# Moving two row-sum matmuls down TensorE's order, and rounding the weight block A22 ahead of the differences S3 and S4

## The chip, the cores and the metric

The kernel runs on one core of a Trainium2 chip. A core has five engines that run side by side and wait for each other by semaphores: TensorE (PE, matmuls and transposes; its weight loads are listed as PEld), VectorE (DVE), ScalarE (ACT), GpSimd (POOL) and SyncE (SP, which issues the DMA transfers). The metric is the device time of one execution in microseconds; the time of a kernel is the median of its runs.

## The reference

One step of a diffusion backbone with one layer. There are 128 context tokens and 512 latent tokens of 1024 features, in float32. What bears on the change:

```python
h = _rms(x, norm_mix) * (1 + sc1) + sh1
proj = h @ w_in                       # q, k, v, and the three conv inputs gb, gc, u
attn = _block_attention(q_r, k_all, v_all)
y_conv = gb * _short_conv(gc * u, conv_w)
merged = concat([_rms(attn, attn_out_norm), _rms(y_conv, conv_out_norm)])
x = x + g1 * (merged @ w_out)
h2 = _rms(x, norm_ffn) * (1 + sc2) + sh2
gate, up = split(h2 @ w_gate_up)      # 1024 -> 2 * 2816
x = x + g2 * ((silu(gate) * up) @ w_down)
```

`_rms(attn, ...)` needs, for each token, the sum of squares of the 512 attention features. It is that sum, for two tiles of tokens, that the change moves.

## The kernel before, in words

**Tokens and precision.** The 640 tokens are five tiles of 128: tiles 0 to 3 latent, tile 4 context. A float32 matmul is done as three matmuls of rounded operands (helper `mm3`, lines 155 to 157): each operand is split into a high half (`wh`, rounded by ScalarE, line 151) and a low half (`wl`, the rest, by VectorE, line 152). High half first, then low half, then TensorE can use the block.

**Who sets the order.** TensorE's order is written out by hand for the whole kernel. For the other engines a scheduler sets the order from dependences and priorities (`early(...)`), except in the first stage, and for VectorE in the opening of the feed-forward part (the block of `f == 0`), where it is by hand too. Tiles come from rings of a few buffers; a new tile waits until the last reader of the buffer it takes is done. Each engine works through its queue strictly in order, so an instruction that waits holds up everything behind it.

**The attention stage** is the list `SEQ`. Its steps:
- `Sn.h`: scores of unit n (one of 16: token tile, key/value head, head pair), head h, on TensorE into a score buffer (line 835); VectorE takes the maximum (841), ScalarE the exponential with its sum (845), then the scaling (847 to 851). There is one score buffer.
- `Tn.g`: transposes of the probabilities of both heads (line 862) into a tile `pt` of the PSUM pool "t", which has two buffers (`PT = 2`); ScalarE and VectorE split it into `ph` and `pl`.
- `On.g`: the product with the values (line 879). After the last one ScalarE copies the result out (886), two DMAs swap halves (894, 895), VectorE adds (900, 901), ScalarE squares into `osq` (902), and GpSimd adds the squares over features in two steps (905, 906).
- `rt`: `att_rms(t)`, line 954. Two passes of a matmul of `osq` with a column of ones give the sums of squares of token tile t, in a tile of the pool "t"; VectorE scales it (line 163, `ms`) and GpSimd takes the power -1/2 (line 165, `rA`). `rA[t]` is first used in the next stage, where the output projection is scaled.
- `F1`: one piece of a filler that runs the conv projections (lines 723 to 725) and the remaining adaLN products (line 394) through the same stage. `Qt`, `qt`: turn and split the queries.

Token tile 0 is finished by unit 3, tile 2 by unit 11.

**The feed-forward part** multiplies the gate and up weights with h2 by Winograd's variant of Strassen's method: 22 blocks f of 128 gate and 128 up columns, of which blocks 0 and 1 are done plainly and blocks 2 to 21 by seven products of 12 matmuls each. In TensorE's order these are A11 B11, S1 T1, S2 T2, A12 B21, S3 T3, S4 B22, A22 T4 (functions `ff_a`, `ff_c`, `ff_d`, `ff_b`, `ff_e`). Between them lie copies on ScalarE that TensorE needs: of the first product (line 1219), of S1 T1 (p5) and S2 T2 (u), line 1212, and after S3 T3 the copy b4 (line 1241), into which A22 T4 is added. The outputs are put together on VectorE (1243, 1246, 1251, 1253) and ScalarE (1225, 1252), and split for the down product (gT).

The raw gate block g(f) and up block u(f) are loaded by SyncE (line 228) into a ring `wf` of three buffers. `op_load` then makes, in the order of `PRODS`:
- "A1": the split of g itself, "A22": the split of half of u;
- "S12": the sums S1 = A21 + A22 and S2 = S1 - A11 on VectorE (line 206) into a tile `sx`, then its split;
- "S34": S3 = A11 - A21 and S4 = A12 - S2 in place in the same `sx` (line 206), then its split.

The halves live in two rings of four buffers, `wh` and `wl`. "A22" takes one buffer, holding both its halves, from `wh` for even f and from `wl` for odd f; the others take one of each. The order of `PRODS` is thus also the order of the rings. Rounding runs ahead of TensorE by up to six entries of that list (`AOP = 6`).

After each group of blocks (0 to 5, 6 to 11, 12 to 16, 17 to 21) comes the down product, whose weights pass through the same rings.

Of the kernel before, what the change touches and what calls it, by code (L numbers as in the profile page):

```python
# [49 lines left out]
GCUT = [0, 6, 12, 17, 22]  # L50
GB = 3
# [40 lines left out]
def build(ctx, tc, x_prompt, x_sample, c, cache_k, cache_v, c_ctx, norm_mix, norm_ffn, w_ada, b_ada,  # L92
# [195 lines left out]
            plan(("ada", 5, j, kp), wa[:, 2 * kp:2 * kp + 2, 5 * D + j * 512:5 * D + (j + 1) * 512], 2, "f")  # L288

    GROUPS = [list(range(a, b)) for a, b in zip(GCUT, GCUT[1:])]  # L290
    PLAIN, PRODS = ("A1", "A2"), ("A1", "S12", "S34", "A22")
    PAIRS = {"A11": ("A1", 0), "A12": ("A1", 4), "A21": ("A2", 0), "A22": ("A2", 4),
             "S1": ("S12", 0), "S2": ("S12", 4), "S3": ("S34", 0), "S4": ("S34", 4)}

# [1038 lines left out]


tile_hymba = with_exitstack(build)

_INS = ["x_prompt", "x_sample", "c", "cache_k", "cache_v", "c_ctx", "norm_mix", "norm_ffn", "w_ada", "b_ada",
# [44 lines left out]
```

## Time and profile before

| | |
|---|---|
| median of 3 runs (lowest to highest) | 755.55 us (754.55 to 755.95) |
| the profiled execution | 756.18 us |
| its span, first to last instruction | 754.4 us |
| TensorE busy | 732.7 us (97%) |
| VectorE / ScalarE / GpSimd busy | 530.2 / 374.9 / 49.5 us |
| granted TensorE clock | 1.00 |
| moved by DMA | 84.50 MB |

The attention stage runs from about 64 to 256 us, the output projection from 256 to 325 us, the feed-forward part from there to the end. In rows of the timeline stand: start, duration, engine, line, operation, output and inputs with the buffer numbers left out, and in brackets the engine's idle time before it and what ended it. In rows of the waits stand: who waited for whom, microseconds in all, times, longest. In rows of the stages: the stage, its length, then busy time and instructions of PE, PEld, DVE, ACT and POOL, the granted clock, the DMA share and GB/s. Matmuls are pipelined, so the durations of neighbours overlap; what counts is the distance of starts.

### The profile page before, as it was taken

Reading aid. Unit: us, or ns where it says so; the run is one execution under the profiler, and the core shown is the slowest. Engines: PE = TensorE matmul, PEld = TensorE weight load, DVE = VectorE, ACT = ScalarE, POOL = GpSimd, SP = SyncE. Lnnn points to the kernel's source line nnn. Section 1 sums busy time; section 2 is a strip of 40 time slices with the busy share of each in tenths; the row PEclk is TensorE's granted clock in tenths of the full one; section 3 lists DMA queues with packets and bytes.
Section 4 is the critical chain, followed back from the end, with each engine's and each line's share of the span. In section 5 each row is a group of like instructions: output and inputs, shape, how many; then the busy total and the mean of one; then the engine's idle time right before and its main releaser. Section 6 shows DMA issues by size and latency. Waiting matters only on the chain.

```text
span 754.4 us, 11635 instructions
## 1 busy us (share of the span) xinstructions
PE 732.7 (97%) x4556; PEld 657.7 (87%) x4556; DVE 530.2 (70%) x905; ACT 374.9 (50%) x701; POOL 49.5 (7%) x85
## 2 busy tenths in 40 slices
PE   7999999999989999999899999999999999999997
PEld 5568878988988887899898799999889998899986
DVE  5558878676656798787868768774568766677653
ACT  5356777677666534775552225553125551255510
POOL 2403101011010120100000000000000000000000
PEclk9999999999999999999999999999999999999999
DMA  9985133533522464031225313233112232123312
GB/s 289 288 244 163 45 109 100 167 93 93 173 92 91 133 226 137 1 112 48 87 91 181 113 56 97 72 99 125 56 56 84 84 112 83 45 72 110 99 70 84
DMA packets 101387, 84.50 MB, mean 112 GB/s; under 512 B 3502, under 2 KB 81650, under 8 KB 101332
## 3 DMA queue, kind: packets, MB, share of 16 engines
q1 hardware_dynamic: 100980, 83.39, 35.9%
q0 software_dynamic: 352, 0.37, 0.3%
q8 instruction: 36, 0.59, 0.3%
q14 instruction: 19, 0.16, 0.1%
HBM read 79.68 MB, written 2.75 MB: 109 GB/s over the span
## 4 chain that ended last, share of the span: by engine, by line
PE 78%; DVE 7%; DMA 6%; ACT 5%; issue 2%; SPq 1%; POOL 1%; ACTq 0%; DVEq 0%
PE pf L155 17%; PE pf L156 17%; PE pf L157 17%; PE pc L723 3%; PE pc L724 3%; PE pc L725 3%; PE ps L835 2%; PE po L879 2%; PE pt L862 2%; DMA es<-t 2%; PE pc L394 2%; DMA af<-in_w_ada_dram 2%; DMA wf<-in_w_gate_up_dram 1%; PE ph L156 1%; PE ph L157 1%
## 5 line engine op out<-in xcount | busy, mean ns | idle before, releaser
L152 DVE TENSOR_TENSOR wl<-wf,wh 128x1024 fp32r<-128x1024 f32 (+1 forms) x58 | 68.7, 1185 | 59.1 <-ACT wh L151 44.6
L151 ACT ACTIVATE wh<-wf 128x1024 fp32r<-128x1024 f32 (+1 forms) x68 | 65.6, 968 | 86.2 <-PE pf L157 45.6
L155 PE MATMUL pf<-B,wh 128*128 128x320 f32 x288 | 89.3, 310 | 0.0
L157 PE MATMUL pf<-B,wl 128*128 128x320 f32 x288 | 89.3, 310 | 0.0
L156 PE MATMUL pf<-B,wh 128*128 128x320 f32 x288 | 89.2, 310 | 0.0
L155 PE MATMUL pf<-T,wh 128*128 128x320 f32 x280 | 86.9, 310 | 2.2 <-ACT pf L1241 1.6
L155 PE MATMUL pf<-wh,gT 128*128 128x512 f32 (+1 forms) x225 | 87.0, 387 | 0.0
L157 PE MATMUL pf<-T,wl 128*128 128x320 f32 x280 | 86.7, 310 | 0.0
L156 PE MATMUL pf<-T,wh 128*128 128x320 f32 x280 | 86.7, 310 | 0.0
L156 PE MATMUL pf<-wl,gT 128*128 128x512 f32 (+1 forms) x225 | 86.6, 385 | 0.0
L157 PE MATMUL pf<-wh,gT 128*128 128x512 f32 (+1 forms) x225 | 86.6, 385 | 0.0
L151 ACT ACTIVATE wh<-sx 128x1024 fp32r<-128x1024 f32 x40 | 42.4, 1060 | 82.9 <-PE pf L157 49.8
L152 DVE TENSOR_TENSOR wl<-sx,wh 128x1024 fp32r<-128x1024 f32 x40 | 48.9, 1224 | 27.4 <-ACT wh L151 23.8
L723 PE MATMUL pc<-hH,wh 128*128 128x320 f32 x192 | 61.2, 319 | 0.0
L724 PE MATMUL pc<-hL,wh 128*128 128x320 f32 x192 | 59.4, 309 | 0.0
L725 PE MATMUL pc<-hH,wl 128*128 128x320 f32 x192 | 59.4, 309 | 0.0
L155 PEld LDWEIGHTS pf<-T,wh 128*128 128x128 f32 x280 | 52.6, 188 | 2.7 <-ACT pf L1241 1.8
L157 PEld LDWEIGHTS pf<-B,wl 128*128 128x128 f32 x288 | 54.1, 188 | 0.1
L155 PEld LDWEIGHTS pf<-B,wh 128*128 128x128 f32 x288 | 54.1, 188 | 0.1
L156 PEld LDWEIGHTS pf<-B,wh 128*128 128x128 f32 x288 | 54.1, 188 | 0.1
L156 PEld LDWEIGHTS pf<-T,wh 128*128 128x128 f32 x280 | 52.6, 188 | 0.0
L157 PEld LDWEIGHTS pf<-T,wl 128*128 128x128 f32 x280 | 52.6, 188 | 0.0
(302 smaller groups left out, 1672.2 us busy)
## 6 DMA issues: line engine op xcount, KB each, us to landing
wf<-in_w_gate_up_dram SPq DMA_DIRECT2D x44, 512.0 KB, 3.8
aw<-in_w_ada_dram SPq DMA_DIRECT2D x24, 512.0 KB, 3.9
wf<-in_w_down_dram SPq DMA_DIRECT2D x20, 512.0 KB, 3.9
wf<-in_w_in_dram SPq DMA_DIRECT2D x18, 512.0 KB, 6.1
af<-in_w_ada_dram SPq DMA_DIRECT2D x32, 256.0 KB, 6.4
x<-in_x_sample_dram SPq DMA_DIRECT2D x8, 512.0 KB, 6.1
wf<-in_w_out_dram SPq DMA_DIRECT2D x8, 512.0 KB, 4.2
wf<-in_w_ada_dram SPq DMA_DIRECT2D x8, 512.0 KB, 3.8
```

Source lines behind the costliest of these rows:

```text
L151: act.activation(hi, src, AF.Copy)
L152: dve.tensor_tensor(lo, src, f32(hi), ALU.subtract)
L155: pe.matmul(out, lh, rh, start=start, stop=False, skip_group_check=more)
L156: pe.matmul(out, lh, rl, start=False, stop=False, skip_group_check=more)
L157: pe.matmul(out, ll, rh, start=False, stop=stop, skip_group_check=more)
L394: pe.matmul(out[CG * g:CG * (g + 1)], cp[:, k], w, start=(k < 4), stop=(k >= KD - 4), skip_group_check=True)
L723: pe.matmul(acc, wh[:, k], hH[k][:, c0:c0 + n], start=(k == 0), stop=False)
L724: pe.matmul(acc, wh[:, k], hL[k][:, c0:c0 + n], start=False, stop=False)
L725: pe.matmul(acc, wl[:, k], hH[k][:, c0:c0 + n], start=False, stop=(k == KD - 1))
L835: pe.matmul(s2[:, g, :320], q, kk[:, v, P + g * 320:P + (g + 1) * 320], start=(i == 0), stop=(i == 1))
L862: pe.transpose(tp[:, i, h], u[3][h][:, kt * P:(kt + 1) * P], ident)
L879: pe.matmul(ov, w, x[:, i].rearrange("p a q -> p (a q)"), start=(g == 0 and i == 0 and n == 0), stop=(last and i == len(kts) - 1 and n == 1))
```

## The change

The step `r0` goes from ahead of S7.0 to behind S7.1 and three F1; the step `r2` from ahead of O12.2 to behind S15.1, ahead of T14.0. `r4` and `r1` stay. In the feed-forward part "A22" is made ahead of "S34".

```diff
-       'O4.2 T5.0 F1 T5.1 S6.1 F1 O5.0 T5.2 O5.1 F1 F1 Q2 O5.2 q3 r0 S7.0 F1 T6.0 T6.1 F1 T6.2 O6.0 '
-       'S7.1 F1 F1 F1 O6.1 F1 O6.2 S8.0 T7.0 T7.1 F1 O7.0 F1 F1 T7.2 S8.1 F1 O7.1 F1 S9.0 F1 T8.0 O7.2 '
+       'O4.2 T5.0 F1 T5.1 S6.1 F1 O5.0 T5.2 O5.1 F1 F1 Q2 O5.2 q3 S7.0 F1 T6.0 T6.1 F1 T6.2 O6.0 '
+       'S7.1 F1 F1 F1 r0 O6.1 F1 O6.2 S8.0 T7.0 T7.1 F1 O7.0 F1 F1 T7.2 S8.1 F1 O7.1 F1 S9.0 F1 T8.0 O7.2 '
...
-       'F1 O11.0 S12.1 T11.2 O11.1 F1 F1 S13.0 O11.2 F1 T12.0 T12.1 F1 O12.0 T12.2 S13.1 O12.1 F1 F1 r2 '
-       'O12.2 S14.0 T13.0 T13.1 F1 S14.1 F1 F1 T13.2 F1 O13.0 F1 O13.1 S15.0 F1 F1 O13.2 S15.1 T14.0 '
+       'F1 O11.0 S12.1 T11.2 O11.1 F1 F1 S13.0 O11.2 F1 T12.0 T12.1 F1 O12.0 T12.2 S13.1 O12.1 F1 F1 '
+       'O12.2 S14.0 T13.0 T13.1 F1 S14.1 F1 F1 T13.2 F1 O13.0 F1 O13.1 S15.0 F1 F1 O13.2 S15.1 r2 T14.0 '
...
-    PLAIN, PRODS = ("A1", "A2"), ("A1", "S12", "S34", "A22")
+    PLAIN, PRODS = ("A1", "A2"), ("A1", "S12", "A22", "S34")
```

## The prediction

> **What bounds the kernel now.** I read the page first, then TensorE's waits, then busy time by stage, and last the timeline around each wait.
>
> ```profile
> span 754.4 us, 11635 instructions
> ...
> PE 732.7 (97%) x4556; PEld 657.7 (87%) x4556; DVE 530.2 (70%) x905; ACT 374.9 (50%) x701; POOL 49.5 (7%) x85
> ...
> q8 instruction: 36, 0.59, 0.3%
> ...
> PE pt L954 <- POOL osq L906: 1.9, 1, 1.9
> PE pf L155 <- ACT pf L1241: 1.6, 1, 1.6
> PE pf L155 <- ACT u L1212: 0.6, 1, 0.6
> ...
> 270.00:300.00 30.00, 29.09 (x122) 22.49 (x121) 28.02 (x46) 12.69 (x25) 2.12 (x2) 1.00 0.52 174
> ...
> 424.00:550.00 126.00, 126.00 (x736) 117.05 (x735) 85.18 (x117) 47.45 (x73) 0.00 (x0) 1.00 0.26 80
> ```
>
> TensorE is busy for 732.7 of 754.4 us, so an edit can only win back idle time of TensorE, 21.7 us in all, or add to it. Three of its waits lie where the edit works: 1.9 us at L954 (the r step of token tile 2), and 1.6 and 0.6 us at the start of the feed-forward part. From 424 us on TensorE has no idle time at all in the stage shown: there the second edit can win nothing and can only lose. Between 270 and 300 us VectorE is busy for 28.02 of 30 us, nearly a bound of its own.
>
> **Part 1: r2 leaves its place.** TensorE's order there is S13.1, O12.1, F1 F1, r2, O12.2, S14.0, T13.0, T13.1, F1, S14.1.
>
> ```profile
> 223.47 0.31 PE L725 MATMUL pc<-hH,wl 128*128 128x320 f32 x1
> 225.64 0.38 PE L954 MATMUL pt<-ones,osq 128*128 128x1 f32 x2 [1.86 <-POOL osq L906]
> ...
> 226.81 1.03 PE L862 MATMUL pt<-ident,pr 128*128 128x128 f32 x8
> 227.60 0.39 PE L723 MATMUL pc<-hH,wh 128*128 128x320 f32 x1
> ...
> 229.62 0.56 PE L835 MATMUL ps<-KA,qT 128*128 128x320 f32 x2 [0.47 <-ACT pr L845]
> ...
> 223.75 0.20 ACT L845 ACTIVATION_READ_ACCUMULATOR pr<-ps,nsr,rq 128x1 f32 x1
> ...
> 224.18 0.83 ACT L849 ACTIVATE pr<-pr,nsr 128x640 f32<-128x640 f32 x1
> ...
> 229.37 0.21 ACT L845 ACTIVATION_READ_ACCUMULATOR pr<-ps,nsr,rq 128x1 f32 x1
> ...
> 226.06 0.16 DVE L163 TENSOR_SCALAR ms<-pt 128x1 f32<-128x1 f32 x1 [1.92 <-PE pt L954]
> ...
> 225.14 0.45 POOL L906 TENSOR_TENSOR osq<-osq 128x128 f32<-128x128 f32 x1
> ```
>
> r2 waits 1.86 us until GpSimd has added up its squares (225.14 + 0.45). Without it O12.2 starts at 223.62, the first matmul slot after 223.47, and S14.0 near 223.99, when the exponential of S13.1 has let go of the score buffer (223.75 + 0.20 and 0.04 of latency). What is late next is T13.0: its second transpose needs the scaled probabilities of S13.1, which ScalarE ends at 224.18 + 0.83 = 225.01. That transpose ran at about 226.91 (226.81 and a tenth: the eight of T13.0 and T13.1 hold TensorE until 227.60) and now runs at 225.05: 1.86 us earlier. The next wait, at 229.62, is for the exponential of S14.0 (229.37 + 0.21), which hangs on ScalarE's split of T13.0 and so moves with it. I take 1.85 us won here, r2's own slot included.
>
> **Part 1b: r2 and r0 at their new places.** r2 now stands between S15.1 and T14.0.
>
> ```profile
> 155.26 0.35 PE L954 MATMUL pt<-ones,osq 128*128 128x1 f32 x2
> 155.48 0.54 PE L835 MATMUL ps<-KA,qT 128*128 128x320 f32 x2
> ...
> 239.85 1.03 PE L862 MATMUL pt<-ident,pr 128*128 128x128 f32 x8
> ...
> 240.05 0.82 DVE L841 TENSOR_REDUCE nsr<-ps 128x1 f32<-128x640 f32 x1 [0.16 <-PE ps L835]
> ```
>
> A pair of r matmuls costs TensorE 155.48 - 155.26 = 0.22 us. But its result sits in the pool "t", which has two buffers: in the built program T14.0 takes one, r2 the other, and T14.1 must wait until VectorE has read r2 (L163). On VectorE that stands behind the maximum of S15.1, 240.05 + 0.82 = 240.87, and takes 0.16 (the row at 226.06), so T14.1 starts at about 241.0. T14.0 and T14.1 ended at 239.85 + 0.79 = 240.64, and now end near 241.0 + 0.40 = 241.4. The place costs 0.75 us; at least the 0.22 of the slot, and at most 1.2 if VectorE is a further half microsecond late. Queued behind the waiting transpose are T14.1 and three F1 steps; ScalarE's split of T14.0 and its exponential of S15.1 go ahead.
>
> r0 had no wait at 155.26 and gets none: its squares are long summed, and T7.1, which now waits for its read, stands six steps further. 0.22 us is saved in one place and paid in the other: 0. **Part 1 in all: -1.85 + 0.75 = -1.1 us**, between -1.6 and -0.6.
>
> **Part 2: A22 is rounded before S34.** No work is added: both halves of A22 cost what they did. What moves is VectorE's and ScalarE's order, the two rings of four buffers (wh, wl), and the loads.
>
> ```profile
> 361.80 0.41 PE L155 MATMUL pf<-T,wh 128*128 128x320 f32 x1 [1.59 <-ACT pf L1241]
> 371.50 0.41 PE L155 MATMUL pf<-T,wh 128*128 128x320 f32 x1 [0.64 <-ACT u L1212]
> ...
> 347.28 0.63 ACT L1073 ACTIVATE T<-tr 128x512 fp32r<-128x512 f32 x1 [0.24 <-DVE tr L1087]
> ...
> 361.33 0.42 ACT L1241 ACTIVATE pf<-pf 128x320 f32<-128x320 f32 x1
> 364.40 1.06 ACT L151 ACTIVATE wh<-sx 128x1024 fp32r<-128x1024 f32 x1 [2.65 <-DVE sx L206]
> ...
> 366.31 0.42 ACT L1219 ACTIVATE pf<-pf 128x320 f32<-128x320 f32 x1
> 366.67 0.61 ACT L151 ACTIVATE wl<-wf 128x512 fp32r<-128x512 f32 x1
> ...
> 369.38 0.74 ACT L151 ACTIVATE gT<-cu 128x640 fp32r<-128x640 f32 x1 [1.42 <-DVE cu L1253]
> 370.06 1.06 ACT L151 ACTIVATE wh<-sx 128x1024 fp32r<-128x1024 f32 x1
> 371.03 0.42 ACT L1212 ACTIVATE u<-pf 128x320 f32<-128x320 f32 x1
> ...
> 348.37 0.68 DVE L1074 TENSOR_TENSOR T<-tr,T 128x512 fp32r<-128x512 f32 x1
> ...
> 351.51 0.68 DVE L206 TENSOR_TENSOR sx<-wf,sx 128x512 f32<-128x512 f32 x1
> ...
> 355.20 0.69 DVE L152 TENSOR_TENSOR wh<-wf,wh 128x512 fp32r<-128x512 f32 x1
> 357.90 0.69 DVE L206 TENSOR_TENSOR sx<-wf 128x512 f32<-128x512 f32 x1 [2.02 <-DMA wf<-in_w_gate_up_dram]
> ...
> 361.46 1.23 DVE L152 TENSOR_TENSOR wl<-sx,wh 128x1024 fp32r<-128x1024 f32 x1 [1.12 <-ACT wh L151]
> 362.60 0.48 DVE L1243 TENSOR_TENSOR cu<-pf,p 128x320 f32<-128x320 f32 x1
> 363.00 0.68 DVE L206 TENSOR_TENSOR sx<-wf,wf 128x512 f32<-128x512 f32 x1
> 363.60 0.69 DVE L206 TENSOR_TENSOR sx<-wf,sx 128x512 f32<-128x512 f32 x1
> ...
> 352.26 5.62 DMA wf<-in_w_gate_up_dram
> ...
> 364.35 3.88 DMA wf<-in_w_gate_up_dram
> ...
> L228 SPq DMA_DIRECT2D aw<-in_w_ada_dram x2: 373/397/421, 244.5 to 245.0; - x2
> DMA to landing us min/median/max: 3.9/4.3/4.7
> ```
>
> The wait at 361.80 runs back so: the copy L1241 (361.33) stands on ScalarE behind the rounding of S12 for f=3, that behind its sums (VectorE, 357.90), those behind the load of u(3), issued at 352.26 and landed at 357.88. It was issued when the second difference of S34(2) had freed g(2)'s buffer (351.51 + 0.68 = 352.19). In the changed program u(3) goes into u(2)'s buffer, freed by the low half of A22(2), which now stands at 351.51 in VectorE's order and takes 0.69 (the row at 355.20): 352.20. Its high half, 0.61 (the row at 366.67), slips in on ScalarE ahead of T2's rounding at 347.28, which had 0.24 to spare: T2 is rounded by 347.28 + 0.37 + 0.63 = 348.28, before VectorE wants it at 348.37, so VectorE's order keeps its times. The chain behind it is the same, so the 1.59 us stay: 0, unless the load's length changes (rivals).
>
> The wait of 0.64 at 371.50 is for the copy u (371.03), behind S12(4)'s rounding (370.06), behind the split of cu (369.38), which had waited 1.42 us for L1253, queued on VectorE behind u(4)'s landing. In the changed order L1253 stands ahead of it. Step by step: VectorE is free at 362.60; A22(3) low 0.60 (the pitch of 363.00 to 363.60); first difference 363.20 to 363.89. It frees u(3)'s buffer, so u(4) is issued at 363.95 instead of 364.35 and lands after 3.88 at 367.83. Second difference to 364.49; ScalarE rounds S34 from 364.5 (was 364.40) and copies L1219 at 366.4 (was 366.31; TensorE needs it at two products after 363.6, 367.1). L1243, L1246 and L1251 take 0.4 each to 365.6, S34's low half 1.15 to 366.8, L1253 ends near 367.75. ScalarE: split of cu 367.8, p5 copy, S12(4)'s rounding when u(4)'s two sums are done, 367.85 + 0.60 + 0.69 = 369.2, copy u 370.2 to 370.6. TensorE is free for it at 371.50 - 0.64 = 370.86. The wait goes: **-0.64 us**, with 0.2 us to spare; nothing is late next, since the earlier loads draw f=4 forward as well. Between nothing and -0.64.
>
> Later units: between the two waits lie five products, 370.86 - 361.80 = 9.06, 1.8 us each. In the rings the changed program lets no rounding start later than four products, 7.2 us, before its first use, and one takes 1.06 + 1.23 us. This cover hides the swap; gone, it would cost each unit what it is short by.
>
> **Sum.** -1.1 - 0.64 = -1.74 us. The profiled execution took 756.18 us, 1.8 outside its span of 754.4, and lies 0.63 above the median of 755.55. It would take 754.4; the median becomes **753.8 us**. A measurement of this kernel tells about 0.2%, 1.5 us, from no change: that bound lies at 754.04, and the forecast just beyond it.
>
> **Rivals.** *Absorbed.* The stage at 270 to 300 us is almost full on VectorE. If its start hangs on loads that do not move with TensorE, part 1 is lost there and only 0.64 stays: 754.9. For: 28.02 of 30 us busy. Against: the work that leads into it follows TensorE's last units. 0.18.
>
> *Shorter load.* 5.62 us is long beside 3.88 for a load of the same size, and instruction blocks come in on the same engines (0.59 MB in 36 packets). If u(3) no longer meets one, it lands 1.7 us sooner and the 1.59 go too: 752.2. Against: it is issued at the same point of TensorE's order. 0.12. [...]
>
> *Loads that collide.* g(4) is now issued at about 352.85, right behind u(3), instead of after 355.9 (A22's low half at 355.20), and g(5) right behind u(4). If two loads share the engines, each first one lands later, by up to the largest lateness the rows show, 5.62 - 3.88 = 1.74 us. The first delay goes whole onto the wait at 361.80 (+1.74); the second makes the wait at 371.50 one of 1.74 - 0.24 = 1.5 instead of 0.64 (+0.86): -1.1 + 2.6 = +1.5, 757.05, right at the upper bound. It decides once u(3) lands after 359. Against: two loads of adaLN weights (aw) issued 0.5 us apart (244.5 and 245.0) landed after 3.9 and 4.7 us, the first undelayed. 0.10. [...]
>
> *Rings too short, the slower side.* A22 takes a ring slot ahead of S34, so in each second unit S34's half waits for a matmul block that ends one product later than before. If queues on ScalarE and VectorE eat the room of 7.2 - 2.3 = 4.9 us, TensorE waits at S3T3 of every unit: 0.3 us in each of the 18 from f=4 on is +5.4 - 1.74 = +3.7, 759.2. It decides at a queue of 4.9 us; the longest that the rows show for such a rounding is 2.65 (364.40), at the tight start. 0.10.
>
> That the change does not do what it says is no rival: in the built order r0 and r2 have moved and A22 stands ahead of S34 in every unit.
>
> **Numbers.** Forecast 0.50 (its own range 753.2 to 754.5, 0.35 of it beyond the bound), absorbed 0.18, shorter load 0.12, collision 0.10 (half of it beyond the upper bound), rings 0.10. Faster 0.35 + 0.11 = 0.46; slower 0.05 + 0.10 = 0.15; the rest, 0.39, within the bound. The range leaves out collision and rings, 0.20: 751.9 to 755.7.
>
> **What would show it.** Right: no wait at L954; a wait of about 0.5 us of a transpose L862 for VectorE's L163 near 239 us; the wait for L1241 still 1.6 and none for u L1212; none after 372 us. Wrong: a wait for L1241 above 2.5 (collision) or gone (shorter load), new waits for L155 on wh or wl in later units (rings), or waits at 288 to 293 us grown by about 1 (absorbed).

## The result, and the profile after

The changed kernel takes **751.76 us** (median of 6 runs, 751.38 to 752.85) against 755.38 for the kernel before on the same chip (6 runs, 753.87 to 755.95). The ratio is 0.9959, 95% interval 0.9946 to 0.9971: faster by 0.41%, beyond the 0.2% that this measurement tells from no change. The medians differ by 3.6 us, the ratio says 3.1 (2.2 to 4.1), where 1.74 was forecast; on the forecast's scale, 0.9959 of 755.55 is 752.45, inside its range. The profiled execution took 752.85 us.

The page after, then its waits of TensorE, then three of its stages:

```profile
span 751.1 us, 11645 instructions
...
PE 732.7 (98%) x4556; PEld 657.4 (88%) x4556; DVE 529.0 (70%) x905; ACT 374.8 (50%) x701; POOL 49.2 (7%) x85
```
```profile
PE pc L394 <- DMA af<-in_w_ada_dram: 1.9, 3, 1.2
...
PE ph L156 <- DVE wl L252: 0.7, 2, 0.4
...
PE pt L862 <- DVE ms L163: 0.4, 1, 0.4
```
```profile
270.00:300.00 30.00, 29.35 (x129) 22.96 (x128) 27.70 (x45) 13.23 (x27) 2.12 (x2) 1.00 0.50 165
345.00:372.00 27.00, 26.99 (x183) 26.48 (x182) 24.02 (x36) 16.56 (x29) 0.00 (x0) 1.00 0.29 80
424.00:550.00 126.00, 126.00 (x734) 116.91 (x734) 83.79 (x116) 47.54 (x73) 0.00 (x0) 1.00 0.28 84
```

TensorE's work is the same 732.7 us; only idle time went. None of the three waits that the prediction named is listed any more: L954, L1241 and u L1212 do not stand among the waits of TensorE, and from 345 to 372 us TensorE is busy for 26.99 of 27 us. One wait is new, the 0.4 us of a transpose (L862) for VectorE's L163. From 270 to 300 us nothing got worse, and from 424 to 550 us TensorE still has no idle time. The opening (L394) was 0.7 us worse in this execution; in a second profile of the same kernel (e7 in the table below) the opening is earlier than in the profile of before, so this is the execution's and not the change's.

The timeline after, at r2's new place and at the second of the two feed-forward waits:

```profile
238.03 0.46 PE L835 MATMUL ps<-KB,qT 128*128 128x320 f32 x2
238.32 0.28 PE L954 MATMUL pt<-ones,osq 128*128 128x1 f32 x2
238.46 0.64 PE L862 MATMUL pt<-ident,pr 128*128 128x128 f32 x4
239.47 0.66 PE L862 MATMUL pt<-ident,pr 128*128 128x128 f32 x4 [0.37 <-DVE ms L163]
...
355.02 0.69 DVE L206 TENSOR_TENSOR sx<-wf 128x512 f32<-128x512 f32 x1 [0.42 <-DMA wf<-in_w_gate_up_dram]
...
364.48 0.49 DVE L1253 TENSOR_TENSOR cu<-cu,cg 128x320 f32<-128x320 f32 x1 [0.44 <-ACT cg L1252]
365.03 0.69 DVE L206 TENSOR_TENSOR sx<-wf 128x512 f32<-128x512 f32 x1
...
367.52 0.42 ACT L1212 ACTIVATE u<-pf 128x320 f32<-128x320 f32 x1
...
367.53 0.31 PE L156 MATMUL pf<-B,wh 128*128 128x320 f32 x1
367.68 0.31 PE L157 MATMUL pf<-B,wl 128*128 128x320 f32 x1
...
367.99 0.19 PEld L155 LDWEIGHTS pf<-T,wh 128*128 128x128 f32 x1 [0.27 <-ACT u L1212]
...
368.00 0.42 PE L155 MATMUL pf<-T,wh 128*128 128x320 f32 x1
```

T14.1 waits for L163, as forecast. L1253 now runs ahead of u(4)'s sum (365.03) on VectorE, the copy u ends at 367.94, and the product starts with no wait listed for its matmul. It does not start early, though: its weight load had waited 0.27 us for the copy, and it starts 0.32 us behind the matmul before it (367.68), where 0.15 is usual. So about 0.17 us of the wait is left, where the forecast had 0.2 to spare. What was not forecast stands in the fifth row: u(3)'s sum starts at 355.02, after a load of 4.0 us instead of 5.62.

Where the time went is best seen by comparing the same matmuls. The table is worked out from the traces: by how much TensorE starts the same matmul later (+) or earlier (-) than in the profile of before, near the time given in its column (times of the profile of before). A change from one column to the next is what that stretch gained or lost. The lower rows are the experiments' profiles.

```
profile             150    180    224    232    252    300    355    363    373    750
after             +0.61  +0.25  +0.25  -1.52  -0.77  -1.27  -1.27  -2.88  -3.49  -3.34
e7 after again    -0.51  -0.87  -0.86  -2.70  -1.94  -2.35  -2.35  -3.94  -4.70  -4.55
e5 before again   -0.58  -0.58  -0.59  -0.56  -0.58  -1.04  -0.87  -2.72  -2.45  -2.45
e6 before third   -1.08  -1.08  -1.08  -0.37  -0.37  -0.84  -0.43  -2.28  -1.96  -1.97
e9 before timed   -0.50  -0.50  -0.50  +0.29  +0.82  +0.79  +0.77  -0.62  -0.42  -0.42
e1 r only         +0.13  -0.23  -0.23  -2.06  -1.30  -1.81  -1.82  -3.21  -2.95  -2.96
e2 A22 only       -0.29  -0.29  -0.28  +0.40  +0.38  -0.05  -0.05  -1.57  -2.15  -2.15
e3 r2 later       -0.67  -1.03  -1.02  -2.87  -2.66  -2.88  -2.89  -4.62  -5.19  -5.19
e4 no spin        -0.40  -0.40  -0.39  -0.34  -0.37  -0.73  -0.74  -2.58  -2.26  -2.26
e8 r2 in wait     -0.59  -0.95  -0.95  -2.85  -2.87  -3.38  -3.38  -4.95  -5.65  -5.65
e10 in wait, no spin +0.41 +0.05  +0.06  -1.74  -1.75  -2.25  -2.27  -3.95  -4.62  -4.63
e11 wait filled   +0.08  +0.08  +0.07  +0.13  +0.10  +0.33  +0.32  -0.73  -0.60  -0.60
```

For after: r0 gains 0.36 (150 to 180), the wait for GpSimd 1.77 (224 to 232), r2's new place costs 0.75 (232 to 252), a stretch of the output projection gains 0.50 (252 to 300; e5 and e6, the unchanged kernel, gain 0.46 and 0.47 there, so most of it is not the change's), the wait for L1241 goes for 1.61 (355 to 363) and the one for u for 0.61 (363 to 373).

### The profile page after: what moved, and what is told of

It is laid out like the page before. It is cut to its first block, busy times and chain, and to the rows that moved or that the text cites. A ratio compares the mean times of both kernels' runs of the same rounds, so it can differ in the third digit from the quotient of the medians.

```text
span 751.1 us, 11645 instructions
## 1 busy us (share of the span) xinstructions
PE 732.7 (98%) x4556; PEld 657.4 (88%) x4556; DVE 529.0 (70%) x905; ACT 374.8 (50%) x701; POOL 49.2 (7%) x85
## 4 chain that ended last, share of the span: by engine, by line
PE 85%; DVE 4%; ACT 4%; DMA 4%; issue 1%; SPq 1%; POOL 0%; ACTq 0%
PE pf L155 19%; PE pf L156 19%; PE pf L157 19%; PE pc L723 3%; PE pc L725 3%; PE pc L724 3%; PE po L879 2%; PE pt L862 2%; PE ps L835 2%; PE pc L394 2%; PE ph L156 2%; PE ph L157 2%; PE ph L155 2%; DMA af<-in_w_ada_dram 1%; SPq L329 1%
```

## The experiments

### Each part alone, r2 at a third place, and other instruction blocks

**e1**: only `SEQ` as in the changed kernel.

```diff
-    PLAIN, PRODS = ("A1", "A2"), ("A1", "S12", "A22", "S34")
+    PLAIN, PRODS = ("A1", "A2"), ("A1", "S12", "S34", "A22")
```


> Only r0 and r2 move; A22 stays behind S34. The prediction's part 1 gives -1.1 us on 755.4, so 754.3; read from the trace of the kernel after (wait of 1.86 gone, a wait of 0.37 new) it is -1.5, so 753.9. The waits at the start of the feed-forward part tell the theories on the load of u(3) apart. Theory 'block': in the kernel before a 16 KB instruction block (queue q8, 355.72 us, 0.96 us long) came in on one of the 16 DMA engines in front of that engine's last packets of u(3); whether it does is settled by a few tenths between the block and the load's issue, which the order of A22 does not set. Then the wait for L1241 may be here or gone, and its load has 5.6 us exactly where a q8 packet lies inside it and is followed by packets of u(3). Theory 'order': A22 ahead of S34 is what shortens the load; then here, with S34 ahead, the wait for L1241 is still 1.6 and the load 5.6 us.

Measured: 753.22 us, ratio 0.9971 (0.9961 to 0.9982), -2.2 us (-2.9 to -1.4).

**e2**: the kernel before with only that line as in the changed kernel.

```diff
-    PLAIN, PRODS = ("A1", "A2"), ("A1", "S12", "S34", "A22")
+    PLAIN, PRODS = ("A1", "A2"), ("A1", "S12", "A22", "S34")
```

> Only the order of rounding changes; r0 and r2 stay. The prediction's part 2 gives -0.64 us: 754.8, with the wait for L1241 (1.6) still there and the one for u L1212 gone. Theory 'order': both go, -2.2 us, 753.2, in this kernel too. Theory 'block': the wait for L1241 goes with the load of u(3) alone, so 754.8 if a q8 packet lies in front of its last packets and 753.2 if not; the wait for u L1212 is gone either way.

Measured: 754.74 us, ratio 0.9991 (0.9978 to 1.0004), -0.7 us (-1.7 to +0.3).

Waits of e1, then of e2:

```profile
PE pf L155 <- ACT u L1212: 0.9, 1, 0.9
...
PE pt L862 <- DVE ms L163: 0.4, 1, 0.4
...
PE pf L155 <- ACT pf L1241: 0.2, 1, 0.2
```
```profile
PE pt L954 <- POOL osq L906: 1.7, 1, 1.7
```

The wait for u belongs to the order of A22: with the old order it stands (0.9), with the new one it is gone though r2 has not moved. The wait for L1241 belongs to neither: it is 0.2 in e1 and not listed in e2. That fells the theory "order". Together the two parts make -2.9, about the whole. The time of e2 is not told from no change. It is the -0.64 of the forecast and not the -2.2 that the theory "block" gives for a run in which the wait for L1241 goes too: a first sign that the kernel before seldom has that wait.

**e3**: the changed kernel with r2 three F1 later.

```diff
-... S15.1 r2 T14.0 T14.1 F1 F1 F1 T14.2 ...
+... S15.1 T14.0 T14.1 F1 F1 F1 r2 T14.2 ...
```


> The kernel after with r2 placed three F1 steps later, ahead of T14.2 instead of T14.0, so that T14.1 no longer needs the buffer that r2 holds. If the wait for VectorE's L163 (0.37 in the trace) is the whole cost of the place beside r2's slot of 0.2, it goes and the time is 0.4 us below that of the kernel after: 751.4. Rival: the wait only brings the next one forward (the transposes T14.1 then wait for nothing, but the scores of the next unit or VectorE's full stage at 270 to 300 us take it up): no difference, 751.8.

Measured: 752.20 us, ratio 0.9963 (0.9948 to 0.9977). The place costs 0.21 instead of 0.75 in the table, and the wait for L163 is gone; but the time does not tell it from the changed kernel, so the gain of 0.4 us that was expected is not shown by time.

**e4**: the kernel before without the four idle matmuls `d4` behind `m0` in the opening order `P1SEQ`.

```diff
-... e21d x3 m0 d4 w e30a ...
+... e21d x3 m0 w e30a ...
```


> The kernel before, without the four idle matmuls on the identity (8 in the trace, 15.23 us) that TensorE runs in the opening just ahead of a wait of 1.05 us for ScalarE; it leaves out nothing of the result. TensorE's order then has 16 instructions fewer ahead of everything behind. Theory 'block': 36 blocks of 16 KB for 4556 matmuls and 4556 weight loads are a block for every 253 of TensorE's instructions, so each block now falls 8 matmuls, about 1.2 us, later: at 356.9 us instead of 355.7, when u(3) has all its packets. The load takes about 4 us, the wait for L1241 falls from 1.6 to nothing, and the time falls by up to 1.6 us, to 753.8, with neither part of the change made. Rival: the load is long for another reason (queue, memory, its buffer): 755.4, wait and load as before.

Measured: 754.39 us, ratio 0.9987 (0.9977 to 0.9998), -1.0 us (-1.7 to -0.15). u(3) lands after 3.7 us; g(4), issued 355.5, after 5.6, with the block at 358.6, and nobody waits for it. The load of u(3) and the wait are as the theory "block" has them, though the block came at 358.6 and not at the 356.9 that it gave. The time alone is no proof of it, as the next runs show.

### Is the wait for L1241 a trait of the kernel before?

**e5, e6**: the kernel before, unchanged, two more profiles. **e7**: the changed kernel again. **e8**: r2 where TensorE waits anyway.

```diff
-... T13.0 T13.1 F1 S14.1 ... S15.1 r2 T14.0 ...
+... T13.0 T13.1 F1 r2 S14.1 ... S15.1 T14.0 ...
```


> The kernel before, unchanged, for a second profile. In the first, the instruction block reached the last of the 16 DMA engines 0.26 us before it would have been through with u(3) (11 of 1024 packets left behind the block), and none of five profiles of other kernels shows that. Theory 'toss': the load of u(3) takes 5.6 us in some executions and about 4 in others, as a few tenths fall; where it takes about 4 the wait for L1241 is gone, the wait for u L1212 is 0.9 to 1.0 instead of 0.6, and the execution is 1.3 us shorter. Rival 'trait': the kernel before always has it: load 5.6, wait 1.6.

> The kernel before once more, for a third profile. Theories and numbers as for the second.

> The kernel after, unchanged, for a second profile and for times on the same chip as the next kernel. If the wait for L1241 is a toss here too, it may show 1.6 in this profile; the r steps' rows must repeat: r0's old place free, its new one 0.22, T14.1's wait for L163 0.37. Time 751.8 against 755.4 of before.

> The kernel after with r2 between T13.1's F1 and S14.1, where TensorE waits 0.46 us for the exponential of S14.0 anyway. If r2 costs what the ledger of the traces says, its 0.17 at the place ahead of T14.0 and the 0.59 behind it go, and its slot of 0.2 falls into the 0.46: 0.75 us below the kernel after, 751.0. Rival: r2 takes the buffer of T13.0, whose low half VectorE reads late, and so begins a wait of its own longer than 0.46: no gain or a loss, 751.8 or above.

Measured: e5 753.74 and e6 754.22 us (one execution each); e7 751.89, ratio 0.9953 (0.9936 to 0.9971); e8 **750.95**, ratio 0.9939 (0.9923 to 0.9954).

No trait, then: in e5 and e6, and in e9 below, u(3) lands after 3.7, 3.7 and 4.2 us and the wait for L1241 is 0.2 at most. Of four profiles of the kernel before only the first has it. Its transfers show why: first the packets of u(3) up to 355.71 us with the load's row, then the next 0.95 us.

```profile
q1 hardware_dynamic: 1028, 0.52, 51.1%
...
wf<-in_w_gate_up_dram SPq DMA_DIRECT2D x1, 512.0 KB, 5.6
```
```profile
q8 instruction: 1, 0.02, 6.3%
```

Packet by packet, the 1028 are 1013 of the load's 1024 packets of 512 B and 15 of the 16 four-byte words that close it, read here as one for each of the 16 DMA engines. Then comes one 16 KB instruction block, 0.96 us long, and no packet of the load at all: the last 11 stand behind it on one engine, 0.26 us (11 of 23.5 ns) short of the end, and then take 0.62 us. In e4, where the block falls into g(4), it again has exactly 11 packets of that load behind it on one engine. In e1, e2, e9 and after all 16 engines had closed the load when the block came, 3.5 to 3.7 us behind its issue, and it starts within 0.02 us of the last closing word; in before it came 3.46 us behind the issue. In e5 and e6 it came 3.0 us behind it, when 8 of the 16 engines had closed, and, as the load was not late, to one that had. So a few tenths, and the engine that the block falls to, decide how late the load is. What sets them is not shown: 11 packets twice, and a block right behind the close four times, do not look like chance. In e11 below the block comes ahead of the first packet of u(3), which lands after 4.6 us, and the wait for the copy b4 (L1241, L1244 in that kernel) is 0.5. Whether the order of A22 bears on it stays open: a load of 5.6 us stands in one of seven profiles with the old order and in none of six with the new one.

In e8 r2 stands in a wait that shrinks instead of growing, and the place ahead of T14.0, where the changed kernel has it, is free again:

```profile
226.15 0.28 PE L954 MATMUL pt<-ones,osq 128*128 128x1 f32 x2
226.78 0.56 PE L835 MATMUL ps<-KA,qT 128*128 128x320 f32 x2 [0.34 <-ACT pr L845]
...
236.99 1.04 PE L862 MATMUL pt<-ident,pr 128*128 128x128 f32 x8
```

The exponential of S14.0 ended 0.46 us after TensorE was free in the profile of after, and with r2 in front the rest is 0.34. The table has nothing lost from 232 to 252. By the medians of e7 and e8, which ran side by side, this is 0.9 us below the change as made, about the 0.75 that the table shows; but the intervals of the two ratios overlap, so the time does not tell the two apart.

### Does the comparison lean, and do blocks cost the changed kernel?

**e9**: the kernel before, timed against itself. **e10**: e8 with the diff of e4 as well.

> The kernel before, unchanged, timed against itself and profiled a fourth time. By the ledger of the traces the r steps are worth 0.36 + 1.78 - 0.76 = 1.4 us and the order of A22 0.9 to 1.0, 2.3 in all, but the medians say 3.6 to 4.0, and two of three profiles of the kernel before (753.7, 754.2) lie 1.5 us under its median. If the comparison leans (the kernel that is timed against before gains by its place in the round), the ratio here is about 0.998; if not it is 1.000 within 0.0015. In the profile: a load of u(3) of 3.7 to 4.2 us and no wait for L1241, or the toss of 5.6 and 1.6 again.

> The kernel with r2 ahead of S14.1 (750.95 us), and without the idle matmuls in the opening, so that the instruction blocks fall at other places of TensorE's order. In the kernel before that gave -1.0 us and runs closer together. If the blocks' tosses cost the changed kernel as much, it gives 1.0 here too: 750.0. If A22's order has already taken the load of u(3) out of their reach (g(4), behind it, is what comes late, and nobody waits for it), it gives nothing: 751.0.

Measured: e9 755.41 us, ratio 0.9994 (0.9981 to 1.0007): no lean. e10 751.20, ratio 0.9939 (0.9922 to 0.9957), as e8: shifting the blocks gives nothing here.

e9's table row shows something new. From 224 to 252 us, at r2's old place, TensorE loses 1.32 us against the first profile; e6 loses 0.71 and e2 0.66 at the same place, and none of the six profiles with r2 moved loses anything there. No wait is listed for it. The stages of e9, cut where the clock's records of that trace change, and three of its matmuls:

```profile
222.71:226.12 3.41, 1.63 (x12) 1.36 (x12) 0.32 (x2) 2.01 (x5) 1.58 (x3) 1.00 0.02 5
226.12:229.53 3.41, 3.41 (x16) 3.37 (x15) 2.18 (x3) 2.17 (x6) 0.15 (x1) 0.50 0.00 0
229.53:232.95 3.42, 3.42 (x26) 2.39 (x25) 2.23 (x5) 1.58 (x6) 0.00 (x0) 1.00 0.00 0
```
```profile
225.06 0.38 PE L954 MATMUL pt<-ones,osq 128*128 128x1 f32 x2 [1.78 <-POOL osq L906]
...
228.53 0.47 PE L725 MATMUL pc<-hH,wl 128*128 128x320 f32 x1
...
229.72 0.31 PE L724 MATMUL pc<-hL,wh 128*128 128x320 f32 x1
```

The third number from the end of a stage's row is the granted clock: 1.00, then 0.50 for 3.41 us, then 1.00, and a matmul of the same shape takes 0.47 instead of 0.31. The wait of 1.78 us lies wholly in the stretch before, which is left with 1.63 us of work. The first profile of before, cut into stretches of the same 3.41 us that are counted from the first clock record of its own trace (the raster: that record, at 1.00, runs for 747.52 us, 219 times 3.413; the one of after for 744.11, 218 times), is cut differently:

```profile
221.83:225.24 3.41, 1.95 (x14) 1.68 (x12) 1.19 (x3) 2.54 (x6) 0.83 (x2) 1.00 0.02 5
225.24:228.66 3.42, 3.02 (x23) 3.01 (x24) 1.57 (x3) 1.60 (x5) 0.90 (x2) 1.00 0.00 0
```

There 1.46 us of the wait fall into one stretch and 0.40 into the next, and the clock stays. The six profiles with r2 in its old place agree: 1.70, 1.72 and 1.78 us in one stretch (e2, e6, e9) are followed by a drop, 1.46, 1.46 and 1.06 (before, e5, e4) by none.

That border holds at this place only. In the opening the clock falls to 0.50 for one stretch in e1, e4, e5 and e11, each time behind a stretch with 1.38 to 1.54 us of idle time, and for two in e10, behind one with 1.91. The first two rows are e4's opening, the others the first profile of before at the wait for L1241:

```profile
16.24:19.65 3.41, 2.03 (x6) 1.05 (x6) 3.29 (x6) 1.85 (x3) 0.93 (x2) 1.00 1.21 290
19.65:23.07 3.42, 3.42 (x24) 2.00 (x24) 1.08 (x3) 0.00 (x0) 3.42 (x7) 0.50 1.15 318
```
```profile
358.36:361.78 3.42, 1.86 (x13) 1.59 (x11) 2.30 (x4) 1.38 (x2) 0.00 (x0) 1.00 0.16 46
361.78:365.19 3.41, 3.39 (x23) 3.39 (x24) 3.30 (x6) 0.79 (x1) 0.00 (x0) 1.00 0.00 0
```

Behind 1.38 us of idle time in e4 the clock falls, behind 1.56 in before it does not, and at the end of e9 a stretch with 1.76 (748.36 to 751.77) brings no fall either. So idle time within a stretch bears on the fall, but how much of it is needed is not shown, and it does not decide alone.

### Filling the wait

**e11**: the kernel before, with idle matmuls in r2's wait.

```diff
-        sps = PB((P, 1))
+        sps = PB((P, P))
+        for _ in range(6 if t == 2 else 0):
+            pe.matmul(sps, ident, ident, start=True, stop=True)
+        sps = sps[:, 0:1]
```


> The kernel before, with r2 in its old place, and ahead of r2's matmul six idle matmuls of the identity with itself (12 in the trace, about 1.6 us) that fill most of its wait of 1.86; the result leaves nothing out. Theory 'clock': in three of six profiles with r2 in its old place the granted clock fell to 0.5 for one stretch of 3.41 us right behind the wait, each time where 1.70 to 1.78 us of the wait lay within one such stretch, and not where 1.46 or less did; it made TensorE 0.7 to 1.3 us later each time, 0.45 on the mean. With the wait filled the clock stays 1.00 at 224 to 232 us, and the time is 0.45 below that of before though nothing ends earlier: 755.2, with runs closer together. Rival: the drop has nothing to do with the wait: a granted clock of 0.8 at 224 to 232 us in about half of the executions, 755.6 as before. The instruction blocks fall some 1.8 us earlier behind this place, so the load of u(3) may meet one at another point.

Measured: 755.16 us, ratio 0.9991 (0.9981 to 1.0002), -0.7 us (-1.4 to +0.15). 0.6 us of r2's wait is left, and the clock stays:

```profile
224.00:232.00 8.00, 6.93 (x54) 5.85 (x52) 4.05 (x8) 4.29 (x10) 1.73 (x3) 1.00 0.00 0
```

Eleven of its twelve runs lie between 754.74 and 755.81 (the twelfth took 757.67), where before spreads from 754.29 to 757.15. That is what the theory "clock" expects, but the interval just reaches no change and one profile can't show that the drop never comes: it fits, it is not proved by time.

## Why the prediction was right, and where it was too small

**The stall at L954, -1.85.** Right: 1.77 in after, 1.84 in e7, 1.83 in e1, and what came next was late as forecast (S14.1's scores wait 0.5 for the exponential as before). Missing from the term was the clock behind the wait. In three of six profiles with r2 in its old place the granted clock fell to 0.5 behind it, which cost 0.66 to 1.32 us; over the four profiles of before that is 0.5 on the mean. In the six profiles with r2 moved and in e11, with the wait filled, it did not fall there. That the wait brings the fall rests on these counts and is not proved.

**r2's new place, +0.75.** Right in size and kind: 0.75 and 0.76 in the table, 0.17 of it up to 240 us and the rest by the wait for L163, which was listed as 0.37 where about 0.5 was said. e3 and e8 take the pool's wait away and, in the table, win most or all of it back.

**r0, 0.** Wrong: -0.36 in each of the profiles where it moved. The step that failed is "r0 had no wait at 155.26": none of the matmul engine's, but its weight load had one. Before, and then the same place after:

```profile
154.85 0.28 PE L879 MATMUL po<-pl,VS 128*128 128x256 f32 x1
155.23 0.30 PEld L954 LDWEIGHTS pt<-ones,osq 128*128 128x128 f32 x2 [0.30 <-issue]
155.26 0.35 PE L954 MATMUL pt<-ones,osq 128*128 128x1 f32 x2
155.45 0.30 PEld L835 LDWEIGHTS ps<-KA,qT 128*128 128x128 f32 x2
```
```profile
155.47 0.28 PE L879 MATMUL po<-pl,VS 128*128 128x256 f32 x1
155.47 0.31 PEld L835 LDWEIGHTS ps<-KA,qT 128*128 128x128 f32 x2
155.59 0.46 PE L835 MATMUL ps<-KA,qT 128*128 128x320 f32 x2
```

From L879 to L835 TensorE took 0.63 us with r0 and 0.12 without, about the slot of 0.22 and the 0.30 in which the weight load was held up at issue. By the next matmuls TensorE is 0.59 us earlier there, and at the new place r0 costs 0.22. The row names nothing that the weight load waited for, so why it was held up stays open. The slot was read from the start of r0 to the start of what follows; it should have been read from the start of what comes before.

**The wait for u L1212, -0.64.** Right, and by the steps given: L1253 goes ahead of u(4)'s sum, and the wait is not listed for the matmul in after, e2, e3, e7, e8 and e10, and stands in e1, e4, e5, e6, e9 and e11. The 0.2 us to spare was not there: about 0.17 of the wait is left in after, and in five of these six profiles the weight load still waits 0.2 to 0.3 for the copy. It was sized in an odd execution: where u(3) is not late, the wait is 0.8 to 1.0 with the old order, and the two stretches from 355 to 373 us are some 0.95 shorter with the new order (2.10 to 2.35 us below the first profile in six profiles, against 0.92 to 1.58 in six with the old order and without the late load).

**The wait for L1241, 0.** It went, as the rival "shorter load" said, and for its reason, an instruction block in front of the load's last packets. But the rival took it, as the forecast did, for a property of the kernel before that the change keeps or removes. It was one execution's: it costs 1.3 us net (the wait for u grows when it goes) in one profile of four. The sign that was named for it, a wait still of 1.6, failed. In eleven of the 13 profiles the wait for L1241 is 0.2 us at most; in the first profile of before it was 1.6, and in e11 0.5 (L1244 there), with a block inside the load in the one and ahead of it in the other.

**The other rivals.** Nothing was absorbed from 270 to 300 us. The loads did not collide: u(3) took 4.0 with g(4) right behind it. The rings held: no wait from 372 us on.

**The sum.** Over the profiles (four of before; after and e7), leaving out the opening, which differs from execution to execution: r0 -0.36, r2's old place -2.2 with the clock in it, the new place +0.6, the output projection -0.2, 300 to 355 us -0.1, L1241 -0.3, u -0.9, a late +0.15: -3.3 us, where the medians say -3.6 and -4.0. The forecast of -1.74 is the sum of its three terms; with r0, the clock and the ordinary size of u it would have been about -2.9. By time alone, the 752.45 measured lies nearer to the rival "shorter load" (752.2) than to the forecast (753.8), and it is inside the range because that rival was taken into it. The mechanisms of the three terms were right; that the whole came out inside the range, with a gain at r0 and one at the clock that were not in the sum, is in part luck. What stays open: how often the clock falls and the load is late, for which four profiles are few, and why e4 gained 1.0 us, when the late load is worth 0.3 on the mean and r2's wait stands in e4.

## What to carry to other kernels

Before a wait is priced, see whether it stands in a second profile of the same kernel: of the three waits here one was that execution's alone. In three of six profiles the granted clock fell behind r2's wait, and that cost 0.66 to 1.32 us beside the 1.7 to 1.8 of the wait itself, so removing a wait may be worth more than its row says. A small step that must stand somewhere can be free where TensorE waits for another engine anyway (r2 in e8: nothing lost from 232 to 252 us, against 0.75 in after), and its price is read from the start of the instruction before it, with the weight loads' rows, to the start of the one behind (r0: 0.63 us with it, 0.12 without).

## What the runs showed of the hardware

- **The granted clock fell after stretches of 3.41 us with 1.38 to 1.91 us of idle time.** Its changes in before, after and e9 lie on a raster: its record at 1.00 runs for 747.52 us in before and 744.11 in after, 219 and 218 times 3.413, and its record at 0.50 in e9 for 3.41. In the 13 profiles it falls to 0.5 eight times ahead of the kernel's end, for one stretch (two in e10), each time after a stretch with 1.38 (e4) to 1.91 us (e10) of idle time in it; after other stretches with 1.46, 1.56 and, at the end of e9, 1.76 us it did not. At 0.50 a matmul of 128x320 took 0.47 us, at 1.00 0.31 (e9).
- **Instruction blocks came in among a load's packets.** 36 blocks of 16 KB work out to one for every 253 of TensorE's 9112 matmuls and weight loads; between neighbours lie 152 to 361 of them in before and 204 to 301 in after, and the block near u(3) comes behind 4481 of them in both. In the first profile of before each block is one packet of 0.9 to 1.3 us (one took 2.2), and a load that still had packets behind one landed late (u(3) in before, 11 packets, 5.6 us; g(4) in e4, 11 packets, 5.6).
- **Of two loads issued 0.6 us apart, the first was undelayed** (u(3) in after, 4.0 us). The second landed after 6.4 us with a block behind the first, and after 5.1 in the next pair, where no block came.
